# 359 displacements in the issue order of a two-layer encoder on one core

## The chip, the cores and the metric

The kernel runs on one core of one Trainium2 chip. The metric is the device time in microseconds of one execution. Three runs of the kernel before took 1170.71, 1170.90 and 1170.93 us, median 1170.9 us. One more execution was profiled: it took 1170.47 us, and its span from the first to the last instruction of the program is 1168.7 us, so 1.8 us lie around the span.

## The reference: what is computed

A two-layer encoder trunk over 1024 tokens of 1024 features, in float32. Each layer is an adaLN-modulated RMS norm, a token mixer, and a gated residual; a final RMS norm follows.

```
for layer in range(2):
    shift, scale, gate = split(silu(c) @ ada_w[layer] + ada_b[layer], 3)
    h = rms_norm(x, norm_w[layer]) * (1 + scale) + shift
    y = even_mixer(h) if layer == 0 else odd_mixer(h)
    x = x + gate * y
return rms_norm(x, final_norm)
```

- Layer 0 has two head groups side by side. Group A: 8 query heads on 2 key heads, 64 wide, normed and rotated, dense softmax over all 1024 keys. Group B: 8 latent heads (query rank 256, key/value rank 128, a shared 32-wide rotary key), dense softmax. Both are gated by SiLU and go through one output product.
- Layer 1 has 16 heads on 4 key heads in a window of 128 tokens to either side, with a distance penalty and a sink logit per head, gated by SiLU, and an output product.

## The kernel before, in words

Precision is kept by splitting: an operand is a rounded high part (fp32r) and the remainder, so that a product is two or three matmuls. A tile of attention therefore goes round all engines: PE writes scores S into PSUM, DVE takes the negated row maximum `nm`, ACT exponentiates into `Pa` (group A), `Pb` (group B) or `p` (layer 1) and sums, DVE takes the reciprocal, POOL scales, PE transposes four 128x128 blocks of it against `ident` into one PSUM bank, ACT copies the high part into `hla`, `hlb` or `hl`, DVE subtracts the low part into the second half of the same tile, and PE multiplies both halves with V (`VA`, `VB`, `V`). A group of four query blocks is a unit (`a00` to `a71`, `b00` to `b71`); the next unit's scores are issued among the transposes and value products of the unit before. Projections of gates (`wg`, `gps`), the preparation of group B (`qrt`, `qrl`, `VB`) and in layer 1 the query, key and gate projections are filled in between. The reductions `ada` and `adag`, one DVE instruction each over a 512 KB tile of the modulation weights, are spread over the whole run. The output products (`wino_out`) use sums of weight blocks that DMAs accumulate in DRAM, and second-pass keys and queries of group B (`k2`, `q2`) are put together by transfers.

No engine's order is written by hand. Every call to an engine goes through a `Recorder`: it keeps an `Op` with an index (the number in the displacements), its engine and the ops that it depends on. `run` lists all 9,580 ops on five engines with an assumed duration for each, `emit` sorts them by the start so found and issues them in that sequence, which fixes the order on every engine: 6,070 matmuls and transposes on PE, 1,485 instructions on DVE, 1,153 on ACT, 557 on POOL, 315 DMAs on SP. Semaphores follow from the dependences, and each engine takes its instructions in the issued order.

Before that, `moved` applies the displacements `MOVES` one after another. `(0, i, j)` takes op i, with those ops that it depends on and that stand between, to just ahead of j; `(1, i, j)` takes op i, with those that depend on it and stand between, to just behind j. `banks_in` then gives a PSUM bank to each accumulator in the new sequence, the old one where it is free. In the kernel before `MOVES` is empty. All recorded instructions carry the one line of `emit` that issues them (L551 before), so the profile tells them apart by tiles.

Of the kernel before, what the change touches and what calls it, by code (L numbers as in the profile page):

```python
# [69 lines left out]
ADA_AT = (8, 5, ("c2", 6), 2, 4, 10, ("op", 1, 7), ("w", 2, 2))  # L70


MOVES = ()

SLOPES = [float(np.float32(2.0) ** np.float32(-8.0 * k / 16)) for k in range(1, 17)]

# [37 lines left out]
class Recorder:  # L114
# [428 lines left out]
    def emit(self):  # L543
        total = self.run()
        real = lambda v: v.real() if isinstance(v, VP) else v
        seq = self.moved([o.i for o in sorted(self.ops, key=lambda o: (o.start, o.i))], MOVES)
        self.banks_in(seq)
# [1518 lines left out]
```

## Time and profile before

| what | value |
|---|---|
| median of 3 runs | 1170.9 us |
| profiled execution, its span | 1170.47 us, 1168.7 us |
| mean granted clock of PE | 0.995 of 2.4 GHz |
| busy in the span: PE, DVE, ACT, POOL | 1135.8, 933.0, 697.5, 592.1 us |
| instructions | 17,585 |

A row of the timeline gives start, duration, engine, operation, the tile written and those read, and a count. The duration of a matmul runs to a modelled end and overlaps the next one, so the pace of PE is read from the distance between starts. A bracket at the end of a row says how long the engine was idle before it and what released it.

### The profile page before, as it was taken

The page shows a single profiled execution, that of the slowest core. Times are in us where ns is not written, and L with a number is a line of the kernel's source. Part 1 is how long each engine was busy: PE and PEld are TensorE (multiplying, and loading weights), DVE is VectorE, ACT ScalarE, POOL GpSimd, SP SyncE. Part 2 cuts the span into 40 slices and gives each one's busy share as a digit, 9 for nine tenths or more (in the row PEclk, how much of TensorE's full clock was granted, in tenths as well). Part 3 has the DMA queues.
Part 4 walks back from the last instruction along what each step waited for, and adds up shares of the span by engine and source line. Part 5 has one row for each costly group of instructions (what it writes and reads, how often), then busy time and mean ns, then how long its engine had stood idle before and what let it go on. Part 6 is the DMA issues. An engine that isn't in the chain of part 4 may idle for free.

```text
span 1168.7 us, 17585 instructions
## 1 busy us (share of the span) xinstructions
PE 1135.8 (97%) x6070; PEld 954.9 (82%) x6070; DVE 933.0 (80%) x1662; ACT 697.5 (60%) x1406; POOL 592.1 (51%) x563
## 2 busy tenths in 40 slices
PE   7999999999999999999999999999999999999995
PEld 7898887877888878788887887988888888888785
DVE  7974888888887888788789997858875687776985
ACT  5553366666565777887788823328755466565722
POOL 1334487877865545333435346606456265345424
PEclk9999999999999999999999999999999999999998
DMA  9601458664553251431064335200002112046303
GB/s 369 258 1 55 167 199 228 169 223 118 162 133 96 79 152 40 105 73 54 19 186 187 133 126 186 103 19 19 19 25 87 65 45 89 19 165 235 136 24 144
DMA packets 45641, 137.64 MB, mean 118 GB/s; under 512 B 5488, under 2 KB 10096, under 8 KB 45552
## 3 DMA queue, kind: packets, MB, share of 16 engines
q1 hardware_dynamic: 42160, 127.08, 31.5%
q0 software_dynamic: 2304, 8.39, 4.2%
q8 instruction: 48, 0.79, 0.3%
q10 hardware_dynamic: 1088, 1.05, 0.3%
q14 instruction: 41, 0.34, 0.1%
HBM read 105.43 MB, written 39.45 MB: 124 GB/s over the span
## 4 chain that ended last, share of the span: by engine, by line
PE 81%; DVE 7%; DMA 5%; ACT 3%; issue 1%; POOL 1%; SPq 0%; POOLq 0%; ACTq 0%; DVEq 0%
PE psum L551 81%; DMA ada<-in_ada_t 2%; DVE nm L551 2%; DVE p L551 1%; DMA w2s<-in_w_c 1%; DMA w31s<-in_w_c 1%; DMA o<-spill 1%; DMA xr<-in_xt 1%; ACT Pa L551 1%; DVE hla L551 1%; DVE hlb L551 1%; DVE psum L551 0%; SPq L551 0%; ACT p L551 0%; DVE hT10l L551 0%
## 5 line engine op out<-in xcount | busy, mean ns | idle before, releaser
L551 DVE TENSOR_REDUCE nm<-psum 128x1 f32<-128x1024 f32 x128 | 154.4, 1216 | 17.2 <-PE psum L551 15.7
L551 POOL TENSOR_SCALAR p<-p,dn 128x384 f32<-128x384 f32 (+1 forms) x128 | 72.4, 584 | 156.8 <-DVE dn L551 68.8
L551 POOL TENSOR_SCALAR Pa<-Pa,rs 128x1024 f32<-128x1024 f32 x64 | 76.4, 1210 | 42.7 <-DVE rs L551 29.2
L551 PE MATMUL psum<-hla,VA 128*128 128x512 f32 x256 | 92.9, 421 | 4.4 <-DVE hla L551 2.5
L551 POOL TENSOR_SCALAR Pb<-Pb,rs 128x1024 f32<-128x1024 f32 x64 | 71.9, 1126 | 44.4 <-DVE rs L551 39.2
L551 DVE TENSOR_TENSOR hla<-psum,hla 128x512 fp32r<-128x512 f32 x128 | 83.5, 681 | 12.2 <-ACT hla L551 11.7
L551 ACT ACTIVATE Pa<-psum,nm 128x1024 f32<-128x1024 f32 x64 | 71.8, 1123 | 33.9 <-DVE nm L551 30.9
L551 DVE TENSOR_TENSOR hlb<-psum,hlb 128x512 fp32r<-128x512 f32 x128 | 82.2, 683 | 10.0 <-ACT hlb L551 9.7
L551 PE MATMUL psum<-hlb,VB 128*128 128x512 f32 x256 | 88.9, 424 | 0.6
L551 ACT CAST hla<-psum 128x512 fp32r<-128x512 f32 x128 | 71.5, 597 | 29.7 <-PE psum L551 26.9
L551 PE MATMUL psum<-ident,Pa 128*128 128x128 f32 x512 | 88.2, 272 | 0.6 <-DVE VB L551 0.4
L551 ACT ACTIVATE Pb<-psum,nm 128x1024 f32<-128x1024 f32 x64 | 71.9, 1124 | 25.9 <-DVE nm L551 21.8
L551 PE MATMUL psum<-k,q 128*128 128x512 f32 x256 | 84.6, 401 | 1.4 <-ACT Pb L551 0.8
L551 DVE CUSTOM_DVE_ANT_0 p<-psum,bias,rows_g 128x384 f32<-128x384 f32 (+1 forms) x128 | 69.7, 579 | 17.4 <-PE psum L551 16.5
L551 PE MATMUL psum<-ident,Pb 128*128 128x128 f32 x512 | 79.5, 272 | 0.8 <-DVE og('0', 7)_1192 L551 0.8
L551 ACT ACTIVATE p<-p,nm 128x384 f32<-128x384 f32 (+1 forms) x128 | 74.0, 585 | 2.3 <-DVE nm L551 2.3
L551 ACT COPY ot<-psum 64x512 f32<-64x512 f32 x64 | 37.4, 584 | 60.8 <-PE psum L551 60.3
L551 PEld LDWEIGHTS psum<-ident,Pa 128*128 128x128 f32 x512 | 64.0, 140 | 11.6 <-DVE VB L551 1.2
L551 ACT CAST hlb<-psum 128x512 fp32r<-128x512 f32 x128 | 69.4, 603 | 5.9 <-PE psum L551 5.5
L551 PEld LDWEIGHTS psum<-ident,Pb 128*128 128x128 f32 x512 | 63.0, 140 | 11.3 <-DVE og('0', 7)_1192 L551 1.1
L551 DVE TENSOR_TENSOR hl<-psum,hl 128x512 fp32r<-128x512 f32 x88 | 55.6, 684 | 10.5 <-ACT hl L551 10.1
L551 ACT CAST hl<-psum 128x512 fp32r<-128x512 f32 x88 | 46.2, 592 | 27.7 <-PE psum L551 23.7
(891 smaller groups left out, 3612.0 us busy)
## 6 DMA issues: line engine op xcount, KB each, us to landing
ada<-in_ada_t SPq DMA_DIRECT2D x32, 512.0 KB, 7.0
ws<-in_w_out POOLq DMA_DIRECT2D x16, 512.0 KB, 8.1
adag<-in_ada_t SPq DMA_DIRECT2D x16, 512.0 KB, 4.2
S<-ws SPq DMA_DIRECT2D x16, 512.0 KB, 4.5
o<-spill SPq DMA_DIRECT2D x12, 512.0 KB, 5.3
A<-in_w_out SPq DMA_DIRECT2D x12, 512.0 KB, 5.3
xT<-in_xt SPq DMA_DIRECT2D x8, 512.0 KB, 8.2
ws<-in_w_out SPq DMA_DIRECT2D x8, 512.0 KB, 8.3
```

Of the source, the lines that this page charges most:

```text
L551: fn(*[real(v) for v in a], **{k: real(v) for k, v in kw.items()})
```

## The change

The table `MOVES` gets 359 entries; nothing else differs. Instructions, their operands and their number are the same on every engine. Of 6,070 PE instructions 1,331 stand at another rank (at most 52 ranks away), of 1,485 on DVE 231 (at most 12), of 1,153 on ACT 54 (at most 6), of 557 on POOL 68 (at most 7), of 315 on SP 9 (at most 2). 56 of 872 PSUM accumulators get another bank. No engine's order differs in the last 21 us of the trace.

```diff
-MOVES = ()
+MOVES = (
+    (0, 711, 679), (1, 710, 624), (0, 79, 3), (1, 0, 48), (1, 13, 15), (1, 14, 13), (1, 15, 482), (1, 491, 461),
...
+    (1, 3401, 3398),
+)
```

Three places, each before and then changed. The first is ACT in layer 1, where the copies `hl_230`, `hl_231`, `hl_232` (high parts for the value product of one window block) meet the exponentials `p_25` of the block two further on. Before:

```order
L551 ACTIVATE nm_1638<-nm_1638 128x4
L551 ACTIVATE p_250_1639,dn_1641<-p_250_1639,nm_1638 128x384 x2
L551 ACTIVATE p_251_1640,dn_1641<-p_251_1640,nm_1638 128x384
L551 CAST hl_230_1622<-psum 128x512
L551 CAST hl_231_1623<-psum 128x512
L551 CAST hl_232_1624<-psum 128x512
L551 ACTIVATE p_251_1640,dn_1641<-p_251_1640,nm_1638 128x384
L551 CAST hl_240_1634<-psum 128x512
```

Changed:

```order
L612 CAST hl_230_1622<-psum 128x512
L612 ACTIVATE p_250_1639,dn_1641<-p_250_1639,nm_1638 128x384
L612 CAST hl_231_1623<-psum 128x512
L612 ACTIVATE p_251_1640,dn_1641<-p_251_1640,nm_1638 128x384
L612 CAST hl_232_1624<-psum 128x512
L612 ACTIVATE p_251_1640,dn_1641<-p_251_1640,nm_1638 128x384
L612 ACTIVATE nm_1638<-nm_1638 128x4
L612 ACTIVATE p_250_1639,dn_1641<-p_250_1639,nm_1638 128x384
L612 CAST hl_240_1634<-psum 128x512
```

The first copy went ahead of the small exponential and all four large ones, and the other two copies stand between them.

The second is DVE in group A of layer 0, around the low parts `hla` of unit a01 (339 to 345 are its tiles 1 to 7) and a modulation reduction `ada`. Before:

```order
L551 TENSOR_TENSOR hla_339<-psum,hla_339 128x512
L551 ISA ada_337,mods<-ada_337,cb,cols 128x1024
L551 ISA mods 128x1
L551 RECIPROCAL rs_361<-sm_360 128x1
L551 TENSOR_TENSOR hla_340<-psum,hla_340 128x512
L551 TENSOR_TENSOR hla_341<-psum,hla_341 128x512
```

Changed:

```order
L612 TENSOR_TENSOR hla_343<-psum,hla_343 128x512
L612 TENSOR_TENSOR hla_344<-psum,hla_344 128x512
L612 TENSOR_TENSOR hla_345<-psum,hla_345 128x512
L612 ISA ada_337,mods<-ada_337,cb,cols 128x1024
L612 ISA mods 128x1
L612 TENSOR_TENSOR hla_367<-psum,hla_367 128x512
```

The reduction went behind the six low parts that stood behind it.

The third is PE in group A, where the first value product of unit a41 (`hla_594` with `VA`) follows scores of unit a50 (`khh`, `kll` with `Qa_456`). Before:

```order
L551 MATMUL psum<-khh_194,Qa_456 128x512
L551 MATMUL psum<-kll_196,Qa_456 128x512
L551 MATMUL psum<-hla_594,VA_105 128x512 x2
L551 MATMUL psum<-ident,Pa_562 128x128
L551 MATMUL psum<-ident,Pa_566 128x128
```

Changed:

```order
L612 MATMUL psum<-ident,Pa_574 128x128
L612 MATMUL psum<-ident,Pa_562 128x128
L612 MATMUL psum<-ident,Pa_566 128x128
L612 MATMUL psum<-ident,Pa_570 128x128
L612 MATMUL psum<-ident,Pa_574 128x128
L612 MATMUL psum<-kll_196,Qa_456 128x512
L612 MATMUL psum<-ident,Pa_562 128x128
L612 MATMUL psum<-ident,Pa_566 128x128
L612 MATMUL psum<-ident,Pa_570 128x128
L612 MATMUL psum<-ident,Pa_574 128x128
L612 MATMUL psum<-hla_594,VA_105 128x512 x2
```

Eight transposes that stood behind the value product now stand ahead of it.

## Rows read from the trace of the kernel before

**Rows 1.** The page, busy time: engine, busy us, share of the span, instructions.

```profile
PE 1135.8 (97%) x6070; PEld 954.9 (82%) x6070; DVE 933.0 (80%) x1662; ACT 697.5 (60%) x1406; POOL 592.1 (51%) x563
```

**Rows 2.** The page, the chain that ended last, by engine.

```profile
PE 81%; DVE 7%; DMA 5%; ACT 3%; issue 1%; POOL 1%; SPq 0%; POOLq 0%; ACTq 0%; DVEq 0%
```

**Rows 3.** Windows: stretch, length, busy by engine, PEclk, DMA share, GB/s.

```profile
0.00:45.00 45.00, 38.51 (x197) 34.08 (x198) 38.42 (x62) 25.57 (x33) 3.18 (x9) 0.96 0.97 383
...
143.00:424.00 281.00, 272.24 (x1472) 221.18 (x1471) 242.65 (x382) 181.12 (x334) 203.08 (x196) 1.00 0.56 162
424.00:724.00 300.00, 297.16 (x1569) 245.22 (x1568) 253.26 (x372) 211.67 (x369) 130.59 (x98) 1.00 0.33 104
724.00:1147.00 423.00, 419.92 (x2194) 356.98 (x2193) 320.12 (x728) 230.86 (x544) 199.11 (x213) 1.00 0.24 81
1147.00:1168.70 21.70, 10.41 (x81) 9.22 (x79) 8.55 (x21) 7.12 (x16) 11.49 (x13) 0.79 0.30 101
```

**Rows 4.** Timeline of PE, layer 1, around the value product of hl_230.

```profile
961.99 0.40 PE L551 MATMUL psum<-hT11h,wg1f3l 128*128 128x512 f32 x1
962.22 0.40 PE L551 MATMUL psum<-hT11h,wg1f3h 128*128 128x512 f32 x1
963.85 0.50 PE L551 MATMUL psum<-hl,V 128*128 128x512 f32 x1 [1.24 <-ACT hl L551]
```

**Rows 5.** Timeline of ACT at the same place.

```profile
960.85 0.21 ACT L551 ACTIVATE nm<-nm 128x4 f32<-128x4 f32 x1 [3.72 <-DVE nm L551]
...
963.24 1.53 ACT L551 CAST hl<-psum 128x512 fp32r<-128x512 f32 x3
```

**Rows 6.** Timeline of PE, unit a01 of group A.

```profile
174.96 0.71 PE L551 MATMUL psum<-ident,Pa 128*128 128x128 f32 x5
176.18 0.73 PE L551 MATMUL psum<-hla,VA 128*128 128x512 f32 x2 [0.50 <-DVE hla L551]
```

**Rows 7.** Timeline of DVE at the same place.

```profile
173.56 1.89 DVE L551 CUSTOM_DVE_ANT_0 ada<-ada,cb,cols 128x1024 f32<-128x1024 f32 x1
...
175.46 1.26 DVE L551 TENSOR_TENSOR hla<-psum,hla 128x512 fp32r<-128x512 f32 x2
```

**Rows 8.** Timeline of PE, the last phase of the output product of layer 0.

```profile
723.43 0.50 PE L551 MATMUL psum<-b220h,s40h 128*128 128x512 f32 x1 [0.53 <-DVE xr L551]
```

**Rows 9.** Timeline of PE, first value product of unit a41.

```profile
313.95 0.73 PE L551 MATMUL psum<-hla,VA 128*128 128x512 f32 x2 [0.39 <-ACT Pa L551]
```

**Rows 10.** Timeline of PE, first value product of unit a30 and scores of a31.

```profile
253.54 0.46 PE L551 MATMUL psum<-hla,VA 128*128 128x512 f32 x1 [1.05 <-DVE og('0', 1)_453 L551]
254.42 0.50 PE L551 MATMUL psum<-khh,Qa 128*128 128x512 f32 x1 [0.42 <-ACT Pa L551]
```

**Rows 11.** Windows: the stretch in which group B is prepared.

```profile
386.00:402.00 16.00, 15.27 (x102) 13.16 (x103) 15.37 (x34) 12.82 (x30) 11.43 (x14) 1.00 0.00 1
```

**Rows 12.** Timeline of PE, three of the smaller waits and transposes without a wait.

```profile
183.58 0.50 PE L551 MATMUL psum<-khh,Qa 128*128 128x512 f32 x1 [1.18 <-ACT Pa L551]
...
242.02 0.49 PE L551 MATMUL psum<-ident,Pa 128*128 128x128 f32 x3
242.27 0.49 PE L551 MATMUL psum<-hla,VA 128*128 128x512 f32 x1
243.38 0.50 PE L551 MATMUL psum<-hla,VA 128*128 128x512 f32 x1 [0.61 <-DVE hla L551]
...
462.27 0.49 PE L551 MATMUL psum<-ident,Pb 128*128 128x128 f32 x3
462.79 0.73 PE L551 MATMUL psum<-hlb,VB 128*128 128x512 f32 x2
```

**Rows 13.** Timeline of DVE and POOL, modulation reductions alone and beside POOL.

```profile
12.93 1.34 DVE L551 CUSTOM_DVE_ANT_0 ada<-ada,cb,a 128x1024 f32<-128x1024 f32 x1
...
264.15 2.37 POOL L551 TENSOR_TENSOR wg6l<-wg6s,wg6h 128x1024 fp32r<-128x1024 f32 x1
264.26 3.34 DVE L551 CUSTOM_DVE_ANT_0 adag<-adag,cb,g 128x1024 f32<-128x1024 f32 x1
```

58 rows, old and new, of the table MOVES are left out of this document.

## The prediction

> **What bounds the kernel now.** I read the busy times first, then the chain of work, then the busy time stretch by stretch, and at last the timeline of PE at each of its waits. PE is busy for 1135.8 us of the span of 1168.7 us [rows 1], and 81% of the chain that ended last is its own work [rows 2]. So only time in which PE stands still can be won by another order: 32.9 us at most. The stretches say where it lies [rows 3]. In the first 45 us PE stands for 6.5 us while the DMA engines are busy for 0.97 of the time; after 1147 us it stands for 11.3 us in a tail in which the change moves nothing. Between lie 143 to 424 us with 8.8 us (the dense heads of group A and the preparation of B), 424 to 724 us with 2.8 us, and 724 to 1147 us with 3.1 us: 14.7 us that the change could touch.
>
> That is read a little too low. One matmul of 512 columns starts 0.23 us after the one before it but is shown as 0.40 us long [rows 4], so 0.17 us of each wait is hidden under the modelled end of the instruction before, and the shortest waits have no bracket at all. I therefore take a wait as its bracket plus 0.17. With some sixty waits in the timeline between 143 and 1147 us, that makes up to 25 us.
>
> The Trainium skill (Perfetto Trace Analysis, Identifying the Most-Contended Engine) says that the headroom of PE is not to be judged by matmul busy time, and the trace agrees: 0.40 us shown against 0.23 us of pace.
>
> No wait here is a missing resource for long: DVE is busy for 242.65 of 281 us in the first of these stretches and less after it [rows 3]. PE waits because the one instruction that it needs stands behind others on DVE or ACT, or because PE has its own ready work behind a matmul that isn't ready. Both are a matter of order.
>
> **The change part by part.** The instructions are the same, so nothing is added or taken away but waits. I went through the waits of PE one by one, and looked up in the new order what stands ahead of the waiting matmul and of the instruction that releases it.
>
> 1. The value product of `hl_230` waits 1.24 + 0.17 = 1.41 us [rows 4]. Its high part is copied by ACT at 963.24, behind a small exponential at 960.85 and three large ones, and ACT had been idle for 3.72 us before the small one [rows 5]. Now the copy goes ahead of all of them, 2.4 us earlier. The wait goes: -1.4. The exponentials are 0.5 us later for each copy ahead of them (1.53 for three); their block is transposed two blocks on, so this is hidden.
> 2. The value product of the third tile of a01 waits 0.50 + 0.17 = 0.67 us [rows 6] for a low part that DVE made at 175.46, behind a reduction of 1.89 us [rows 7]. The reduction now stands behind six low parts. The low part is 1.9 us earlier: -0.7. The reduction feeds a modulation column that only layer 1 reads.
> 3. The last phase of the output product of layer 0 waits 0.53 + 0.17 = 0.70 us [rows 8] for DVE to empty a bank. That instruction now passes two DVE instructions of the kind of those at 175.46, 0.63 us each [rows 7], so it is some 1.3 us earlier: -0.7. What it passes makes `hT10l` for products that PE reaches later; if that is late, it costs up to 0.6.
> 4. The first value product of a41 waits 0.39 + 0.17 = 0.56 us [rows 9]. Eight transposes now stand ahead of it, 0.11 us each or 0.9 us: -0.6. A transpose takes 0.11 us since five are shown in 0.71 us and three in 0.49 us [rows 6, 12].
> 5. The scores of a31 wait 0.42 + 0.17 = 0.59 us behind the value product of a30, which itself waited 1.05 us [rows 10]. The exponential that releases them now goes ahead of two copies. The wait of a30 stays, since DVE works through there; I count half: -0.3.
> 6. From 386 to 402 us the order of DVE changes at nine places, small rotary products going behind the `hla` and `VB` that PE waits for. PE stands for 0.73 us, but DVE itself for only 0.63 us [rows 11], and that is the limit: -0.6.
> 7. Fifteen smaller ones, of which rows 12 has three. At 183.58 one matmul of 0.23 us is put ahead (-0.2 of 1.18). At 243.38 three transposes are put ahead and a reciprocal of 0.15 us is passed: -0.5. At 462.79 three transposes take 0.52 us from start to start where at 242.02 three take 0.25, so a wait of 0.27 us without a bracket; five matmuls are put ahead of it, and it goes: -0.3. For the twelve like it I take 0.15 us each (0.05 to 0.35, by the same reading): -1.8. Together 0.2 + 0.5 + 0.3 + 1.8 = 2.8.
>
> What the new order makes worse: where a low part is made after another one (two `hla` of a50 change places), or a score product is put earlier than its bank is free, PE waits for what had slack. I found three places where this exceeds the slack that the trace shows and no longer wait stands just behind; the price of each is between nothing and one DVE instruction, 0.63 us. I take 0.7 in all (0 to 1.9). Other such places, like the scores of the last unit of group A, run into a wait that ends at the same time as before, and cost nothing.
>
> In the first 45 us the DMA engines set the pace (0.97 busy [rows 3]), and the DMAs keep their order but for two pairs of neighbours: 0, and 0.6 us either way at most, one DVE instruction.
>
> The sum: 1.4 + 0.7 + 0.7 + 0.6 + 0.3 + 0.6 + 2.8 = 7.1 won, 0.7 lost, net 6.4. On the profiled execution of 1170.47 us (span 1168.7 and 1.8 around it) this gives 1164.1 us. The median of the runs, 1170.9, is 0.4 higher than that execution, so I forecast 1164.5 us, 0.5% faster.
>
> This adds waits up as if each stood alone. That is right while the other engines follow PE: a wait that goes lets the next transposes start earlier, and so the next copies. It is wrong where DVE or ACT is the one that works without a gap.
>
> **The rivals.**
>
> A. *More goes than I can name.* Of 14.7 us by bracket, or up to 25 by pace, I name 7.1. Moves that only make sense after other moves would show as nothing in my list. If half of the 25 goes: 1170.9 - 12.5 = 1158.4 us, say 1157 to 1161. For it: 359 displacements, of which I tied only some to a wait. Against it: several of the longest waits keep their order, such as the ones at 253.54 [rows 10] and most of 183.58 [rows 12].
>
> B. *DVE gives it back.* In 386 to 402 us DVE is busy for 15.37 of 16 us [rows 11], and PE's wait at 253.54 is for DVE too [rows 10]. If every gain ahead of a long wait for DVE is only waited for there, the repairs of group A (2, 4, 5, 6 and half of 7, 3.6 us) are lost, and 2.8 us remain: 1168.1 us. Against it: DVE has 38 us free in 143 to 424 us [rows 3].
>
> C. *DVE and POOL block each other: slower.* A modulation reduction takes 1.34 us with POOL idle and 3.34 us when it starts 0.1 us after a POOL product of 2.37 us [rows 13]. Six reductions change their place in 143 to 424 us, and POOL is busy for 203 of 281 us there [rows 3]. Each that falls behind a POOL product costs 2.0 us with all low parts behind it. From five on the loss is 10 - 6.4 = 3.6 us: 1174.5 us; from four on the gain is gone. Against it: the reductions were met by POOL before as well (1.89 us [rows 7]), and the one of item 2 now has 1.3 us of idle DVE behind it.
> The Trainium skill (SBUF — State Buffer, Who interferes with whom) says that a DVE instruction with two SBUF inputs and a GpSimd instruction that reads SBUF exclude each other for the whole of whichever started first. The trace agrees: 3.34 us is near 2.37 less 0.1 plus 1.34, that is 3.6. By that rule case C is decided by which engine starts first, which the order alone doesn't tell.
>
> D. *No effect.* 56 accumulators get other banks and so other waits; gains and losses may cancel: 1170.9 us.
>
> **How the numbers follow.** The forecast as worked out (1161 to 1167.5): 0.52. A: 0.14. B (1167 to 1169.5): 0.18. D: 0.08. C: 0.08. For this kernel 0.2%, 2.3 us, is about what a measurement can tell from no change, so faster means under 1168.6 us and slower over 1173.2. Faster: 0.52 + 0.14 + 0.11 of B = 0.77. Same: 0.07 of B and 0.08 of D = 0.15. Slower: C, 0.08. The range reaches down into the half of A and up through B to its end, 1159.0 to 1169.5 us; outside lie D, C and the better half of A, about 0.2.
>
> **What would show it right or wrong.** In the profile of the changed kernel PE's busy time should stay at about 1136 us and its idle time fall by 5 to 6 us, most of it in 143 to 424 us and at the value products of `hl_230` and of a01, where the brackets are gone. The first 45 us and the last 22 us should be the same to within 0.6 us. If the brackets are gone but new ones of the same length stand 10 us later with DVE as the releaser, it was B. If reductions of 2 us and more are seen where there were 1.3, and PE waits for the `hla` behind them, it was C. If waits that I left in place are gone, at 253.54 or 183.58, it was A. My forecast is wrong if the idle time of PE in the middle three stretches falls by under 3 us or over 10.

## The result and the profile after

The changed kernel took 1158.08 us (median of 4 runs, 1157.18 to 1160.08), the kernel before 1170.91 us (4 runs): ratio 0.9892, interval 0.9874 to 0.9909. That is 12.8 us less, where 6.4 were forecast; the time lies 0.9 us below the range. The direction was right, and the gain was twice the forecast.

The page of the changed kernel (engine, busy us, share, instructions), which answers to [rows 1], and its chain, which answers to [rows 2]:

```profile
PE 1129.2 (98%) x6070; PEld 956.4 (83%) x6070; DVE 923.4 (80%) x1662; ACT 696.6 (60%) x1406; POOL 591.0 (51%) x563
...
PE 81%; DVE 5%; ACT 4%; issue 2%; POOL 1%; DMA 1%; SPq 0%; POOLq 0%; ACTq 0%; DVEq 0%
```

The stretches of [rows 3] in the changed kernel, cut where PE has done as many instructions as at the old cuts, the cut at 421.4 twelve later (columns as there):

```profile
0.00:45.00 45.00, 38.78 (x196) 34.41 (x197) 37.89 (x61) 25.25 (x33) 3.01 (x8) 0.96 0.98 383
...
143.00:421.40 278.40, 272.11 (x1484) 223.38 (x1483) 244.52 (x387) 183.43 (x339) 203.61 (x197) 1.00 0.56 163
421.40:714.70 293.30, 292.20 (x1557) 242.69 (x1556) 247.94 (x365) 208.60 (x363) 129.28 (x96) 1.00 0.33 107
714.70:1134.30 419.60, 418.19 (x2194) 357.98 (x2193) 315.06 (x729) 231.29 (x546) 199.56 (x213) 1.00 0.23 81
1134.30:1155.40 21.10, 10.42 (x81) 9.23 (x79) 8.54 (x21) 6.72 (x15) 11.07 (x13) 0.84 0.34 120
```

The span fell by 13.3 us. PE's idle time in the three middle stretches fell from 14.7 to 6.3 + 1.1 + 1.4 = 8.8 us, by 5.9: what the prediction asked for. But PE's busy time fell as well, from 1135.8 to 1129.2, by 6.6 us with the same instructions. Half of the gain was never shown as idle time.

It is seen by pace. From one matmul's end to the next takes 0.11 us at 128 columns, 0.12 at 256, 0.18 at 384 and 0.23 at 512 (medians of both traces; for 512 I allow 0.235). What is over that I call a wait by pace. Between 143 us and the tail there were 59 waits of over 0.1 us, 28.0 us together; now there are 33, 16.1 us. PE's lead is the time at which it had done its first n instructions before, less the same after, at such n where both orders hold the same ones. Worked out from the two traces it grows like this:

| place (us before) | in the forecast | lead won |
|---|---|---|
| 170.5 to 176.7, a01 | item 2: 0.7 | 0.73 |
| 246 to 256, a30 and a31 | item 5: 0.3 | 0.61 |
| 306 to 316, a41 | item 4: 0.6 | 1.00 - 0.79 |
| 386 to 402 | item 6: 0.6 | 1.66 |
| 717 to 724, last phase of layer 0 | item 3: 0.7 | 0.80 |
| 952 to 964, hl_230 | item 1: 1.4 | 1.46 |
| 402 to 415, scores of a71 | no | 1.09 |
| 627 to 637, first units of the output product | no | 1.29 |
| 1092 to 1105, output product of layer 1 | no | 0.91 |
| 233 to 242 and 418 to 420 | no | -0.5, -0.9 |
| all before the last PE instruction | | 12.7 |

The first 45 us lose 0.2. Items 1 to 6 come to 5.5 us, all other places to 7.2: the three rows marked no that gain give 3.3, the last two losses take 1.4, and 5.3 us are small gains, none of over 0.5 us, spread over the run. The last 0.6 us of the 13.3 lie behind PE's last instruction.

Of the 0.9 us lost at 418 to 420 about half is chance. PE waits there for a transfer (`k` from `knp`): by pace 0.57 us in the trace of before, but 0.98 to 1.09 in E3, E10 and E11 below, which have the order of before up to there, and 1.31 to 1.82 in the changed kernel, E6, E9 and E12 to E14, which have the changed one.

### The profile page after: what moved, and what is told of

It is laid out like the page before. It is cut to its first block, busy times and chain, and to the rows that moved or that the text cites. A ratio compares the mean times of both kernels' runs of the same rounds, so it can differ in the third digit from the quotient of the medians.

```text
span 1155.4 us, 17595 instructions
## 1 busy us (share of the span) xinstructions
PE 1129.2 (98%) x6070; PEld 956.4 (83%) x6070; DVE 923.4 (80%) x1662; ACT 696.6 (60%) x1406; POOL 591.0 (51%) x563
## 3 DMA queue, kind: packets, MB, share of 16 engines
q10 hardware_dynamic: 1088, 1.05, 0.3%
## 4 chain that ended last, share of the span: by engine, by line
PE 81%; DVE 5%; ACT 4%; issue 2%; POOL 1%; DMA 1%; SPq 0%; POOLq 0%; ACTq 0%; DVEq 0%
PE psum L612 81%; DVE nm L612 1%; DVE adag L612 1%; DVE hla L612 1%; ACT Pb L612 1%; DVE hlb L612 1%; ACT hla L612 1%; ACT hlb L612 0%; DMA xr<-in_xt 0%; DVE p L612 0%; ACT Pa L612 0%; ACT q L612 0%; POOL r L612 0%; DMA k<-knp 0%; DVE Qa L612 0%
## 5 line engine op out<-in xcount | busy, mean ns | idle before, releaser
L612 PE MATMUL psum<-hla,VA 128*128 128x512 f32 x256 | 89.2, 417 | 2.2 <-DVE hla L612 1.6
L612 PEld LDWEIGHTS psum<-ident,Pa 128*128 128x128 f32 x512 | 63.7, 140 | 14.7 <-DVE gT L612 1.0
```

What stands on the lines that cost most here:

```text
L612: fn(*[real(v) for v in a], **{k: real(v) for k, v in kw.items()})
```

## The experiments

The two sequences differ in 124 stretches, each a rearrangement of its own ops, so any of them can be taken alone. In every experiment the table is replaced by pieces of the sequence written out:

```diff
-MOVES = ()
+PARTS = ((lo, (op, op, ...)), ...)
...
-        seq = self.moved([o.i for o in sorted(self.ops, key=lambda o: (o.start, o.i))], MOVES)
+        seq = [o.i for o in sorted(self.ops, key=lambda o: (o.start, o.i))]
+        for lo, part in PARTS:
+            seq[lo:lo + len(part)] = part
```

Medians in us and ratios to the kernel before (which took 1171.2 to 1171.3 beside them):

| run | order changed in | median | ratio (95%) |
|---|---|---|---|
| E1 | PE alone | 1190.48 | 1.0166 (1.0152 to 1.0180) |
| E2 | DVE, ACT, POOL, SP | 1184.64 | 1.0114 (1.0100 to 1.0128) |
| E3 | one POOL product | 1170.10 | 0.9991 (0.9982 to 1.0000) |
| E4 | PE, DVE, ACT | 1180.54 | 1.0078 (1.0066 to 1.0091) |
| E5 | the named places | 1169.90 | 0.9994 (0.9983 to 1.0005) |
| E6 | all but the named places | 1161.99 | 0.9924 (0.9912 to 0.9935) |
| E7 | DVE and POOL at 624, PE at 411 | 1170.67 | 0.9995 (0.9986 to 1.0003) |
| E8 | PE at 633, ACT at 411 | 1171.24 | 0.9998 (0.9989 to 1.0007) |
| E9 | 143 to 424 us | 1167.12 | 0.9963 (0.9950 to 0.9975) |
| E10 | 424 us to the end | 1162.71 | 0.9928 (0.9915 to 0.9942) |
| E11 | 720 to 760 and 931 to 993 us | 1167.84 | 0.9972 (0.9961 to 0.9982) |
| E12 | all, two places mended | 1157.35 | 0.9881 (0.9868 to 0.9895) |
| E13 | all (the changed kernel again) | 1159.40 | 0.9894 (0.9878 to 0.9911) |
| E14 | all, three reductions moved | 1156.16 | 0.9872 (0.9857 to 0.9886) |

### E1, E2, E4: one engine's part of it

```diff
 E1:  +PE as changed                       DVE, ACT, POOL, SP as before
 E2:  +DVE, ACT, POOL, SP as changed       PE as before
 E4:  +PE, DVE, ACT as changed             POOL, SP as before
```

> TensorE's instructions in the changed order (1331 of 6070 displaced), all other engines in the order before. Theory O (the gain comes from what DVE, ACT and POOL do earlier: the places where the two traces differ and DVE, ACT or POOL was moved, hl_230, a01, the last phase of layer 0, 386 to 402 us, 620 to 637 us and 1095 to 1105 us, give 1.5 + 0.7 + 0.8 + 1.7 + 1.3 + 0.9 = 6.9 us of the 12.8): at most 4 us are won, 1167 us or more. Theory P (the gain comes from PE's own ready work put ahead of waiting matmuls): 8 us or more, 1163 us or less.

> The reverse: DVE, ACT, POOL and SP in the changed order (222 of 231 displaced instructions of DVE, all of ACT and POOL, 7 of 9 of SP), TensorE in the order before. Theory O: 7 us or more, 1164 us or less. Theory P: at most 4 us, 1167 us or more. If the two halves only work together (a matmul put back needs the result made earlier), both stay well short and their gains sum to under 9 us.

> The changed kernel, with POOL (68 instructions) and SP (9) back in the order before; TensorE, DVE and ACT as changed. If a lighter contention of DVE and POOL was won by moving POOL: the 0.9 us at 1095 to 1105 us and up to 1.3 us at 620 to 637 us are lost again, 1159 to 1160.5 us. If POOL's order does not matter: 1158 us. If POOL's order carries most of the extra gain: 1163 us or more.

Each part alone is slower than before, E1 by 19 us, E2 by 13, E4 by 9, which none of the expectations had. The nearest is the last sentence of E2's, that the two halves only work together. PE in E1 at 302 to 326 us and in E2 at 180 to 188 us:

```profile
314.60 0.73 PE L727 MATMUL psum<-khh,Qa 128*128 128x512 f32 x2 [1.51 <-ACT Pa L727]
...
319.05 0.73 PE L727 MATMUL psum<-hla,VA 128*128 128x512 f32 x2 [1.54 <-DVE hla L727]
...
325.54 0.87 PE L727 MATMUL psum<-ident,Pa 128*128 128x128 f32 x3 [2.72 <-DVE Qa L727]
```

```profile
179.96 0.44 PE L688 MATMUL psum<-ident,Pa 128*128 128x128 f32 x2 [1.55 <-POOL Pa L688]
...
188.24 0.50 PE L688 MATMUL psum<-khh,Qa 128*128 128x512 f32 x1 [2.57 <-ACT Pa L688]
```

In E1 the scores at 314.60 stand five places further ahead and wait for the exponential that empties their PSUM bank, which does not. In E2 the exponential that the scores at 188.24 wait for went one place back, and they did not. So neither theory, O nor P, holds: a displacement is one thing over several engines, and one engine's part of it loses.

But not all of the loss is order. `banks_in` gives banks to each of these mixed orders anew: 60 accumulators have another bank than before in E1, 33 in E2, 75 in E4. The value product at 319.05 in E1 has its high part; it waits for the low part because its accumulator now has the bank from which that low part is made, which it has neither before nor in the changed kernel. The longest wait of E4 is of the same kind, a transpose that waits for a low part:

```profile
321.87 0.69 PE L781 MATMUL psum<-ident,Pa 128*128 128x128 f32 x2 [2.02 <-DVE hla L781]
```

Worked out from the orders, the banks and the traces, PE's waits for a bank whose last user before them is another than in either kernel come to 11.1 us by pace in E1, 5.6 in E2 and 13.9 in E4. That each part alone is slower is measured; how much of it is order and how much the new banks is not separated, and E4's loss can't be put down to the order of POOL and SP alone. The experiments below are free of this: E3, E7 and E8 have the banks of before, E12 to E14 those of the changed kernel, and in E5, E6 and E9 to E11 such waits come to 0.2 us at most.

### E3: one displacement on POOL

```diff
 POOL, from 1095 us:
+og130 <- og130, o101
 sq20 <- sq20, sq2001
 sq20 <- sq20, sq2002
 sq20 <- sq20, sq2003
-og130 <- og130, o101
```

> Before, with a single displacement: on POOL the product og130 <- og130, o101 (512 columns) goes ahead of three sums of sq20. Theory O with contention: the product waits at the head of POOL for DVE's o101, so POOL reads nothing while DVE makes o111 (1.58 us before, beside POOL) and o101 (2.20 us); they take 0.7 and 1.2 us, and the two waits of PE at 1103.6 and 1105.0 us (0.49 and 0.42 us by pace) go: 1170.0 us. Rival: PE waits there for the ACT copy or the DMA chain anyway, and nothing changes: 1170.9 us.

DVE and POOL before and in E3, around the sum o101 that PE's t21l needs:

```profile
1098.14 1.58 DVE L551 TENSOR_TENSOR o<-o,og 128x512 f32<-128x512 f32 x1
1099.76 2.20 DVE L551 TENSOR_TENSOR o<-o,o 128x1024 f32<-128x1024 f32 x1
...
1095.43 5.45 POOL L551 TENSOR_TENSOR sq<-sq,sq 128x512 f32<-128x512 f32 x3
```

```profile
1098.82 0.68 DVE L557 TENSOR_TENSOR o<-o,og 128x512 f32<-128x512 f32 x1
1099.53 1.23 DVE L557 TENSOR_TENSOR o<-o,o 128x1024 f32<-128x1024 f32 x1
...
1100.90 1.29 POOL L557 TENSOR_TENSOR og<-og,o 128x512 f32<-128x512 f32 x1 [4.75 <-DVE o L557]
```

As theory O with contention has it: POOL stands for 4.75 us behind an operand that isn't ready, and reads nothing; DVE's two sums take 1.91 us in place of 3.78, and PE wins 0.42 + 0.45 = 0.87 us there. The total is 1.1 us less by the ratio. Its interval ends at 1.0000, but all eleven runs (1169.93 to 1170.89 us) lie below the fastest of before beside them (1170.97). A blocked head of a queue was the gain.

### E5, E6, E11: the named places, the rest, and the surroundings

```diff
 E5:  +9 stretches: 170-191, 250-255 (three), 311-317, 391-402 (two), 720-729, 960-965 us
 E6:  +the other 115
 E11: +14 stretches: 720-760 and 931-993 us
```

> The changed order, all engines, only in the nine stretches that hold the six named items of the prediction (a01 with 183.58, a30/a31, a41, 386 to 402 us, the last phase of layer 0, hl_230); before's order everywhere else. By the working on record these items are worth 4.5 us: 1166.7 us. By the lead that the changed trace gains at these places, if places add up: 5.5 us, 1165.6 us. If a later wait of DVE takes gains back when the rest is not changed too: under 3 us, 1168 us or more.

> The reverse: the changed order everywhere but in those nine stretches. By the working on record the rest is worth 2.6 less 0.7, 1.9 us: 1169.3 us. If places add up, 12.8 - 5.5 = 7.3 us: 1163.9 us. If the unnamed gains hang on the named ones: under 4 us, 1167 us or more.

> The changed order only at 720 to 760 us (the last phase of layer 0 and the start of layer 1) and at 931 to 993 us (around hl_230). With the one stretch of displacements at each place alone PE won 0.84 and 1.35 us there and lost 0.71 and 1.3 us of it within 25 us. Theory neighbourhood: with the neighbours it keeps 0.8 and 1.8 us, together 2.6 us, 1168.7 us. Theory whole: it loses most again, 1170.5 us or more.

E5 wins 0.7 us by its ratio, whose interval takes in 1. Ten of its twelve runs took 1167.4 to 1170.2 us, below every run of before beside them (1170.9 and more); two took 1175.2 and 1175.8, have no profile, and stay unexplained. E6 wins 8.9 us by its ratio. So the places named in the prediction are worth little alone, and those not named carry most.

By PE's lead E5 wins at five of the six places. It keeps what a01 and a30 with a31 give, 1.0 us together, up to 304 us. At a41 it loses 0.9 us where the whole change wins 0.2, and as much again from 332 to 354 us:

```profile
315.29 0.66 PE L585 MATMUL psum<-ident,Pa 128*128 128x128 f32 x4 [0.64 <-ACT Pa L585]
...
353.83 0.50 PE L585 MATMUL psum<-hT00h,wg7h 128*128 128x512 f32 x1 [0.42 <-DVE gT L585]
```

Of 1.5 us won at 386 to 402 us 0.6 are gone by 454 us, and the last two places lose most of theirs right behind. At PE's last instruction 0.2 us of lead are left in this trace. ACT in E5 at hl_230, then PE:

```profile
960.42 0.59 ACT L585 CAST hl<-psum 128x512 fp32r<-128x512 f32 x1 [3.31 <-PE psum L585]
961.43 0.62 ACT L585 ACTIVATE p<-p,nm 128x384 f32<-128x384 f32 x1 [0.42 <-DVE nm L585]
...
964.29 0.61 ACT L585 ACTIVATE p<-p,nm 128x384 f32<-128x384 f32 x1
...
964.89 0.57 ACT L585 CAST hl<-psum 128x512 fp32r<-128x512 f32 x1
```

```profile
962.46 0.39 PE L585 MATMUL psum<-hl,V 128*128 128x512 f32 x1
...
964.47 0.50 PE L585 MATMUL psum<-hl,V 128*128 128x512 f32 x1
965.51 0.50 PE L585 MATMUL psum<-hl,V 128*128 128x512 f32 x1 [0.54 <-ACT hl L585]
```

The wait of 1.24 us [rows 4] is gone (962.46 has no bracket), but the last exponentials, now among and behind the copies, stand ahead of the next copy, `hl_240`, at 964.89, and PE waits for it at 965.51: of 1.45 us won 1.01 are lost. In the full change the stretches beside it mend that: DVE takes the maxima ahead of a sum and its reciprocal, so the first exponential doesn't wait after the first copy, and PE has five gate products (`hT11l`, `hT11h`) ahead of the value product of `hl_240`. ACT and PE of the changed kernel there:

```profile
950.45 0.59 ACT L612 CAST hl<-psum 128x512 fp32r<-128x512 f32 x1 [1.70 <-PE psum L612]
950.93 0.62 ACT L612 ACTIVATE p<-p,nm 128x384 f32<-128x384 f32 x1
...
954.44 0.57 ACT L612 CAST hl<-psum 128x512 fp32r<-128x512 f32 x1
```

```profile
954.37 0.48 PE L612 MATMUL psum<-hl,V 128*128 128x512 f32 x1
954.68 0.71 PE L612 MATMUL psum<-ident,p 128*128 128x128 f32 x5
955.14 0.48 PE L612 MATMUL psum<-hT11l,wg1f3h 128*128 128x512 f32 x1
```

The copy of `hl_240` comes 4.0 us after that of `hl_230` (4.5 in E5), and PE doesn't stand. The neighbours win some of it by themselves: E6, without the stretch at hl_230, still gains 0.7 us there, 0.9 with what follows.

At the last phase of layer 0 E5 wins 0.84 us and loses 0.71 within 10 us, at a wait for a low part of V's weights that DVE now makes later:

```profile
733.53 0.39 PE L585 MATMUL psum<-wv1l,hT10h 128*128 128x256 f32 x1 [0.49 <-DVE wv1l L585]
```

With the stretches around it changed too, E11 keeps 0.7 us here and 1.5 (1.7 with what follows) at hl_230, and is 3.3 us faster by its ratio (2.1 to 4.6 by the interval). So theory neighbourhood, not theory whole, at these two places, in stretches of 40 and 62 us. The other four were not tried with their surroundings alone.

### E7, E8: two places taken apart

```diff
 E7:  +DVE and POOL at 620-627 us;  PE's 22 at 409-413 us
 E8:  +PE's 8 at 632-634 us;        ACT's 2 at 409-413 us
```

> Two places alone. First 620.7 to 626.8 us: 11 instructions of DVE and 3 of POOL as changed, PE and ACT not. Theory contention (b110l, 3.41 us beside POOL's t in before, starts before it and takes 2.2 us): the wait of PE at 634.8 us (1.04 us by pace) goes, 1.0 us won there. Theory PE order: nothing won there. Second 408.7 to 413.4 us: only PE's 22 displaced instructions (the score products of a71 earlier), ACT's two as before. Theory chain (the scores start a chain of DVE maximum, ACT exponential, free bank): the wait at 415.3 us (1.05 us) goes with PE's part alone, 1.0 us won. Theory ACT (the exponential ahead of a copy does it): nothing won. Total 1169.2 us if both are so, 1171.2 us if neither.

> The counterparts: at 632.1 to 633.7 us PE's 8 displaced instructions alone (two transposes ahead of six score products), and at 408.7 to 413.4 us ACT's two alone (the exponential ahead of a copy). Theory contention and theory chain: nothing won at either place, 1171.2 us. Theory PE order: 1.0 us at 634.8 us. Theory ACT: 0.5 us at 415.3 us (a copy takes 0.59 us).

Neither place works by halves. At 634 us the cause is contention: before, POOL's t101 started 0.07 us ahead of DVE's b110l and held it back; in the changed kernel DVE comes first and POOL is the one that waits.

```profile
629.29 3.41 DVE L551 TENSOR_TENSOR b110l<-o,b110h 128x1024 fp32r<-128x1024 f32 x1
...
629.22 2.41 POOL L551 TENSOR_TENSOR t<-o,o 128x1024 f32<-128x1024 f32 x1
```

```profile
622.10 2.22 DVE L612 TENSOR_TENSOR b110l<-o,b110h 128x1024 fp32r<-128x1024 f32 x1
...
623.21 3.36 POOL L612 TENSOR_TENSOR t<-o,o 128x1024 f32<-128x1024 f32 x1
```

In E7 b110l takes 1.74 us and the wait at 634.8 us is gone, as theory contention says. But PE stands at 628 us, where POOL's scaling of Pb now comes behind t100: PE's lead falls by 1.8 us there, comes back by 1.8 at 634, and the place is worth nothing alone:

```profile
628.19 0.33 PE L561 MATMUL psum<-ident,Pb 128*128 128x128 f32 x1 [0.55 <-POOL Pb L561]
629.29 0.33 PE L561 MATMUL psum<-ident,Pb 128*128 128x128 f32 x1 [0.77 <-POOL Pb L561]
```

PE's eight instructions alone (E8) leave the wait at 634 us as it was, 0.78 us by the bracket. At 415 us PE's part alone won 1.05 and lost 1.2 before it, at scores that wait 0.95 us for the exponential `Pa`; ACT's part alone lost 0.7. Together they win the 1.09 us of the table. Theory chain was half right: the scores must come earlier, and the exponential with them.

### E9, E10: do large stretches add up?

```diff
 E9:  +52 stretches from 143 to 424 us
 E10: +67 stretches from 424 us on
```

> The changed order, all engines, only in the stretch of layer 0 from 143 to 424 us. In the changed kernel PE gains 5.2 us of lead there. Theory neighbourhood (a displacement pays only with the displacements within some 10 to 30 us of it, and nothing beyond): all of it stays, 5.2 us, 1166.1 us. Theory whole (gains are waited away again further down unless the rest is changed too): under 3 us, 1168.3 us or more.

> The changed order only from 424 us to the end. In the changed kernel PE gains 7.4 us of lead there. Theory neighbourhood: 1163.9 us, and this run and the one before sum to 12.6 us. Theory whole: the sum of both stays under 9 us.

4.3 and 8.4 us by the ratios (2.9 to 5.9 and 6.8 to 10.0 by the intervals): 12.7 together, and the whole wins 12.6 by its own. (E9 was to win 5.2; its trace has the long adag05 of E13 below, 3.86 us.) Theory neighbourhood holds: what is won in a stretch of some hundred us is not waited away further down. E5 and E6 (0.7 + 8.9 = 9.6 by the ratios, 1.4 + 9.3 = 10.7 by the medians) fall 2 to 3 us short of the whole. That fits with cutting through neighbourhoods, but each of the two is known to some 1.3 us only.

### E12 to E14: reductions that meet POOL

```diff
 E12:       +adag02 (DVE) just ahead of adag03; the stretch at 233-241 us as before, all engines
 E13:        (the changed kernel again)
 E14, DVE:  +adag05 behind hla207, +adag07 behind the third maximum, +adag02 just ahead of adag03
```

> The changed kernel with two places altered. The reduction adag02, which in the changed kernel starts 0.01 us after POOL's wg6l and takes 3.44 us in place of 1.3 while PE waits 1.37 us for the low part hla305 behind it, goes behind hla305 to hla307 and one maximum, just ahead of adag03. And the one stretch at 233 to 241 us, after which adag07 takes 3.74 us and PE loses 0.78 us, goes back to before. If each repair pays what stands there: 1.2 + 0.7 us, 1156.2 us. If the reduction only carries the collision to the next instruction: 1157.5 us or more.

> The changed kernel once more, its order written out. Its runs so far lie 1157.2 to 1160.1 us, more apart than those of the kernel before. Theory toss: the reduction adag05 at 226.8 us meets a row of POOL products; where DVE gets in first it takes 1.29 us (changed kernel's profile), where POOL does 3.9 us (the profiles of three kernels with the same rows there), and PE then waits 1.65 us; so the times fall into groups about 1.6 us apart, and the median is 1157 to 1159.5 us. Rival: the spread is of the DMAs in the first 45 us, and the times spread evenly.

> The changed kernel with three of its modulation reductions on DVE put where fewer POOL products stand: adag05 behind the low part hla207, adag07 behind the third maximum, adag02 behind hla307 and one maximum. Theory toss and collision: adag02 gives 0.8 us (what the run before it kept), adag07 0.8 us (PE's wait at 240.2 us), adag05 nothing against the runs in which DVE came first and 1.6 us against the others: 1155.7 us with runs closer together, under 1 us. Rival: each reduction finds another POOL product at its new place, 1157.5 us or more.

The changed order displaces adag05 to 226.8 us, where POOL has six products in a row. The same rows of DVE and POOL in the profile of the changed kernel, in E13, and E14 (where adag05 comes behind the low parts):

```profile
226.84 1.29 DVE L612 CUSTOM_DVE_ANT_0 adag<-adag,cb,g 128x1024 f32<-128x1024 f32 x1
...
225.88 3.69 POOL L612 TENSOR_TENSOR nrq<-qp,qtab 128x256 f32<-128x256 f32 x5
```

```profile
228.46 3.83 DVE L802 CUSTOM_DVE_ANT_0 adag<-adag,cb,g 128x1024 f32<-128x1024 f32 x1
...
227.47 2.74 POOL L802 TENSOR_TENSOR nrq<-qp,qtab 128x256 f32<-128x256 f32 x5
...
232.95 1.70 PE L802 MATMUL psum<-hla,VA 128*128 128x512 f32 x5 [1.45 <-DVE hla L802]
```

```profile
227.80 2.61 DVE L805 TENSOR_TENSOR hla<-psum,hla 128x512 fp32r<-128x512 f32 x4
230.32 1.88 DVE L805 CUSTOM_DVE_ANT_0 adag<-adag,cb,g 128x1024 f32<-128x1024 f32 x1
```

In one and the same order the reduction takes 1.29 us or 3.83, and PE loses 2.0 us by its lead in the second case. The long time is the usual one: E2, E6, E9 and E12 show 3.86 to 3.91 us there, and only the first profile of the changed kernel the short one. The groups of times 1.6 us apart that theory toss asks for can't be made out in the eight runs of this order. E12, with 3.88, is still 1157.35 us, since adag02 no longer meets `wg6l` (1.27 us in place of 3.44; PE wins 1.6 and gives 1.0 of it back behind). That collision is no fault of the change: before has it too [rows 13].

E14 beside E13: 1156.16 us (1155.68 to 1156.98) against 1159.40 (1157.84 to 1160.17). By PE's lead the two traces differ by 2.0 us at adag05, 0.7 + 0.3 behind adag07 and 0.6 at adag02, 3.4 in all at the end. E14 has the lowest median of all kernels run here, and its runs don't overlap with those of E13; with those of E12 they do. The first theory of E14 forecast 1155.7 us and runs within 1 us of each other; they lie 1.3 us apart.

The rival of E13 is right as well on the place, the start, but not on the cause: the DMA engines are as busy in both profiles (1.03 and 1.02 at 16 to 27 us). What differs is TensorE's granted clock (the column after the counts), in the changed kernel's first profile and in E13:

```profile
16.00:27.00 11.00, 10.66 (x50) 9.29 (x49) 10.38 (x16) 5.73 (x8) 0.00 (x0) 0.88 1.03 407
```

```profile
16.00:27.00 11.00, 9.96 (x40) 8.82 (x41) 10.58 (x17) 5.57 (x7) 0.26 (x1) 0.69 1.02 406
```

At 19 us a matmul of 416 columns starts every 0.19 us in the first and every 0.35 in the second, which is 2.4 and 1.2 GHz. In both PE had stood for over 2 us shortly before (2.72 us to 15.47 in the first, 2.41 to 16.31 in E13). PE loses 1.8 us by it in E13 and 1.7 in E14, which also had 0.69, so the difference between those two is not of the clock. So the first profile of the changed kernel was a lucky one twice, and its runs differ by some 3 us where those of before differ by 1.

## Why the prediction was wrong in size

**Item 1** (1.4): 1.46 in the full change, but its sentence "this is hidden" is wrong. E5 shows what is behind the exponentials on ACT: the next copy, 1.0 us.

**Items 2 and 3** (0.7 each): 0.73 and 0.80. The warning of item 3, up to 0.6 if what is passed comes late, came true in E5 (0.71), for `wv1l` and not for `hT10l`, and is mended by other displacements in the full change.

**Item 4** (0.6): 0.2. The wait went, and one of 0.57 us by the bracket, for `Pa`, came just behind it.

**Item 5** (0.3): 0.6. "The wait of a30 stays" was wrong: 1.05 us [rows 10] became 0.15, with 0.21 at the next value product.

**Item 6** (0.6, capped by DVE's idle time): 1.66. The cap was no cap. DVE was busy there because it was held up by POOL: the sixteen small rotary products (duration min, median, max in ns) fell from a median of 474 to 284. Before, from 383 us on, those with POOL beside them for under 0.1 us took 266 to 283 ns, the others 450 to 1111:

```profile
L551 DVE TENSOR_TENSOR qrt<-qrz,ropeb x16: 266/474/1111, 378.6 to 400.1; 128x128 f32<-128x128 f32 x16
```

```profile
L612 DVE TENSOR_TENSOR qrt<-qrz,ropeb x16: 269/284/829, 375.8 to 396.2; 128x128 f32<-128x128 f32 x16
```

**Item 7 and the loss** (2.8 less 0.7): this is the step that failed. The other places give 7.2 us net where 2.1 were forecast. The prediction looked at what stands right ahead of the waiting matmul and of its releaser, and so had three waits of before, worth 3.3 us, at nothing:

```profile
414.79 0.50 PE L551 MATMUL psum<-khh,Qa 128*128 128x512 f32 x1 [0.78 <-ACT Pa L551]
...
634.49 0.33 PE L551 MATMUL psum<-ident,Pb 128*128 128x128 f32 x1 [0.82 <-DVE og('0', 7)_1192 L551]
...
1103.10 1.21 PE L551 MATMUL psum<-t21h,s21h 128*128 128x512 f32 x4 [0.23 <-ACT t21h L551]
1104.47 0.50 PE L551 MATMUL psum<-t21l,s21h 128*128 128x512 f32 x1 [0.15 <-DVE t21l L551]
```

The releaser came earlier from further back (the scores of a71), or took less time since POOL no longer stood in its way (b110l, o101). The small gains, priced at 2.8 us, come to 5.3; which displacement won each of them was not looked at. The loss was too small as well: the two places of the table take 1.4 us where 0.7 were allowed, and the new waits at 241, 315, 419, 252, 255 and 244 us alone are 0.78 + 0.79 + 0.92 + 0.44 + 0.47 + 0.45 = 3.85 us by pace, part of it within the places of items 4 and 5.

**"Adds waits up as if each stood alone"**: wrong in both directions. Alone the named six give 0.7 us by E5's ratio (1.4 by its median), not 4.5; on top of the rest (12.6 less 8.9 of E6) they give 3.7.

**PE's busy time stays at 1136**: wrong. The idle time fell by 5.9 us as forecast, and the busy time by 6.6. I did add 0.17 us to each named bracket, but forecast the idle time with the full sum, so that its fall by just the 5 to 6 us forecast is luck: the gain was twice as large, and half of it lay inside the busy time. The sign of being wrong, under 3 or over 10 us of idle time, was therefore on the wrong quantity, and would have passed this result. The bound of 25 us by pace was sound; the trace has 28.

**Rivals.** A came true, in time (1158.1, in its 1157 to 1161) and in kind: by pace 11.9 of 28.0 us went, near its half, with waits gone that I had left in place (at 253.54, not at 183.58: 0.78 us of 1.18 is left). It had a chance of 0.14, and the range stopped in the middle of it. Its sentence "moves that only make sense after other moves would show as nothing in my list" is what E5, E6 and E11 show. B is true of single places (E5, where ACT is the releaser as often as DVE), not of the whole (E9, E10). C is true of two reductions: adag07 in all four traces that have the changed order of all engines there, and adag05 in all but the first. Each takes some 2.5 us longer, and PE loses 0.8 and 2.0 us by it:

```profile
234.55 3.74 DVE L612 CUSTOM_DVE_ANT_0 adag<-adag,cb,g 128x1024 f32<-128x1024 f32 x1
```

But I counted contention as a loss only. DVE's busy time fell by 9.6 us, with the same work. D is ruled out: the interval ends at 0.9909.

What stays open: the 0.6 us behind PE's last instruction, where the 5.3 us of small gains come from, how the full change splits between contention and order beyond the places taken apart here, and how the loss of E1, E2 and E4 splits between order and banks.

## What to carry to other kernels

Waits of a matmul engine are to be counted by pace, since here half of them stood inside its busy time. A displacement in a kernel whose work goes round all engines can be worth little without those next to it, on every engine it touches: test a neighbourhood (here stretches of 40 us and more kept what they won), not a single repair or a single engine. Where buffers or banks are given out by the order, look at them too before a loss is put down to the order. And before DVE is called the limit, its durations are to be compared with the shortest of the same shape; at the places looked at here (`qrt`, b110l, o101, the reductions) what was over was POOL, and order could give it back.

## What was not expected of the hardware

A DVE reduction that comes while POOL works through products without a gap mostly isn't let in between them: 3.83 to 3.91 us against 1.27 alone, in E2, E6, E9, E12 and E13; once, in the first profile of the changed kernel, it was let in, and POOL's row took 3.69 us instead of 2.74. The Trainium skill (SBUF — State Buffer, Who interferes with whom) has the one that issues first keep the shared ports for its whole instruction. That a row of short POOL instructions can keep DVE out through its whole length is what these five traces show.

The granted clock at 16 to 27 us was between 0.69 and 1.00 in profiles of kernels whose first 45 us differ little, and 0.88 and 0.69 in two of the very same order, which cost 1.8 us.
